# A five-branch decoder trunk on one core: differential attention ahead of sparse attention, selection rounds spread over both, a signed softmax bias, and paired scores chained in issue

## Chip, core and metric

The kernel runs on one core of a Trainium2 chip. The metric is the device time of one execution in microseconds (us), from the first to the last instruction and what lies around them. The engines are TensorE (PE, with its weight loads as PEld), VectorE (DVE), ScalarE (ACT), GpSimd (POOL) and SyncE (SP, which only issues transfers here).

## The reference, cut to what matters

Two layers. In each, one input projection feeds five branches of 512 tokens by 512 channels; each branch is gated, projected, scaled and summed, and one output projection is added to the residual.

```python
xn = rms_norm(h, norm_g[l])
(a_q, a_k, a_v, i_q, i_k, i_w, b_cq, b_ckv, b_kr, c_q, c_k, c_v, d_u, d_v, e_q, gates, merge) = split(xn @ w_in[l])
branches = (dsa_branch(...),     # A: 8 heads, keys chosen by top-128 of an indexer's score
            mla_branch(...),     # B: 8 heads, latent attention
            diff_branch(...),    # C: 4 head pairs, softmax0 - lam * softmax1, row norm
            sgu_branch(...),     # D: gated chunk mixing
            memory_branch(...))  # E: 4 heads on 256 memory tokens
mixed = sum(sigmoid(merge[:, :, n]) * ((o * silu(gates[:, :, n])) @ w_branch[l, n]) for n, o in enumerate(branches))
h = h + mixed @ w_out[l]
```

Branch A scores all keys with the indexer, keeps the 128 largest per query, and attends with the others masked. Its mask is used as an added tile: 0 where kept, -1e30 elsewhere.

## The kernel before, in words

**Units.** Every float32 product is made of three matmuls on a high and a low part (`three`, L453 to L455; ACT makes the high part of a weight tile at L368, DVE the low one at L371). Projections are "units" which PE works through in the order of the tokens of `ORDER`. After each `three` the unit calls `tick` with 3 x 0.43 ns a column, so a 512-column `three` advances the pacing clock by 0.66 us. By the code a unit lasts, on that clock: a gate `gX#` 10.6 us, a merge `mX#` 15.9 us, each of `a`, `f0`, `f1`, `fv`, `dv`, `du` 21.1 us, `qr`, `q0`, `q1` 4.0 us each, `k0`, `k1`, `v0`, `v1` 2.6 us each, `z` 1.3 us.

**Attention between the units.** `+x` puts a generator (an attention or the indexer) into a queue; it is resumed whenever the pacing clock has advanced by what it last yielded. `-x` runs the rest of it at once, `!x` forces deferred rows. The attentions share the queue `att`; the indexer has the queue `top`. `attend` makes, for each step (head, query block i = 3, 2, 1, 0 with 512, 384, 256, 256 score columns): scores, normalising of the step before, softmax, a pause `PACE[branch]`, transposes of the step before that, a pause, and P times V at the end of a head.

**Selection.** After its scores the indexer does, for query blocks 1, 2, 3, sixteen rounds of `max` (L1007) and `match_replace` (L1008) on 256, 384 and 512 columns, with a pause after each round. `dsa_attention` begins with `pace.finish(S["gidx"])`, which issues whatever rounds are left in one go.

**Banks and buffers.** `psm`: 4 PSUM banks for the units; `psa`: 3 banks for scores (`pS`, `pI`), transposes (`pT`, `pa`) and flips; `pso`: 1 bank for P times V. `pp`: 4 buffers for probabilities. The order on each engine is fixed when the program is built: among the instructions whose inputs and buffers it takes to be ready, the one that comes first in the program is issued, so a later unit's matmuls can go ahead of an attention step which lacks a bank.

**Paired scores.** Branch C computes two heads at once, one on partitions 0 to 63, one on 64 to 127: three matmuls for each, written alternately, into two banks (L1117). **Softmax.** `softmax_head` adds the mask and takes the row maximum in one DVE instruction (L543), turns it into the bias with a second one (L546), and ACT takes the exponential (L548).

Of the kernel before, what the change touches and what calls it, by code (L numbers as in the profile page):

```python
# [11 lines left out]
AF = mybir.ActivationFunctionType  # L12
ALU = mybir.AluOpType
# [10 lines left out]
GONE = -3e38  # L24
# [3 lines left out]
C_DU, C_DV, C_EQ, C_GATE, C_MERGE = 3172, 3684, 4196, 4708, 7268  # L28


ORDER = ("-mem gE0 !ckvt !lat +idx qr q0 !qr0 gE1 k0 v0 +mla0 mE0 q1 k1 mE1 mE2 -mla0 !qr1 v1 +mla1 mE3 a gB0 -mla1 gB1 "
         "!aq +dsa mB0 mB1 mB2 mB3 ws dv f0 z du fv -dsa !df0 +df0 f1 !oD gD0 gD1 mD0 mD1 -df0 !df1 "
         "+df1 mD2 mD3 gA0 gA1 mA0 mA1 -df1 mA3 mA2 gC0 gC1 mem mC0 mC1 mC3 mC2")
NW = 5
NB = 41
NC4 = 6
NTR = 8
NP = 4
NRAW = 4
PACE = {"E": 900.0, "B": 1200.0, "A": 1900.0, "C": 1600.0}  # L40
LAG_ROPE = 5000.0
LAG_QROPE = 10125.0
LAG_RSTD = 4000.0
# [89 lines left out]
def trunk(tc, d, out, taps=None):  # L133
    nc = tc.nc
    V, A, G, T = nc.vector, nc.scalar, nc.gpsimd, nc.tensor
# [29 lines left out]
    def small(n=1, name="sm"):  # L165
        return smp.tile([128, 8], F32, tag="sm", name=name)[:, :n]
# [9 lines left out]

    def f32(ap):
        return ap.bitcast(F32)

    def tap(name, ap):  # L180
        if taps is not None and name in taps:
            nc.sync.dma_start(taps[name], ap)
# [26 lines left out]
    for name in ("mem_norm_g", "norm_g", "sgu_b", "diff_norm_g", "mla_q_norm_g", "mla_kv_norm_g"):  # L209
        src = d[name]  # L210
        n = int(np.prod(src.shape)) // 128
# [328 lines left out]
    def softmax_head(ps, L, mask, scale):  # L540
        p = pp.tile([128, 512], F32, tag="p", name="p")
        m = small(1, "m")
        V.tensor_tensor_reduce(out=p[:, :L], in0=ps[:, :L], in1=mask, op0=ALU.add, op1=ALU.max,  # L543
                               scale=1.0, scalar=GONE, accum_out=m)
        nm = small(1, "nm")
        V.tensor_scalar(nm, m, -scale, None, op0=ALU.mult)  # L546
        s = small(1, "s")
        A.activation(p[:, :L], p[:, :L], AF.Exp, bias=nm, scale=scale, accum_out=s)  # L548
        return p, s

    def normalise(p, s, L):
# [25 lines left out]
    def attend(branch, steps, scores, norm, trans, pv, pv_rows=None):  # L577

        gap = PACE[branch]
        hist = []  # L580
# [66 lines left out]
    def layer(l, mm):  # L647
        w = d["w_in"][l]
        S = {}
# [253 lines left out]
        def ev_k(hf):  # L903
            def ev(ps):
                for m in range(2):
                    for s in range(2):
                        h = 4 * hf + 2 * m + s
                        S["kh"][h], S["kl"][h] = blk(name="kh"), blk(name="kl")
                        rows = slice(64 * s, 64 * s + 64)
                        split(S["kh"][h][rows], S["kl"][h][rows], ps[m][rows])  # L910
                        rr = slice(64, 96) if s == 0 else slice(0, 64)
                        A.activation(S["kh"][h][rr], f32(S["krh"][rr]), AF.Copy)
                        V.tensor_copy(S["kl"][h][rr], f32(S["krl"][rr]))
            return ev

        def ev_v(hf):
# [57 lines left out]
        def indexer():  # L974
            S["iqs"] = [blk(name="iqs") for _ in range(4)]
            for e in range(2):
                to_heads(S["iqs"][2 * e:2 * e + 2], nat_t(128 * e))
                yield 800.0
            S["ki"] = [blk(name="kih"), blk(name="kil")]
            split(S["ki"][0], S["ki"][1], nat_t(256))  # L980
            S["kk"] = [blk(name="kkh"), blk(name="kkl")]
            yield 800.0
            split(S["kk"][0], S["kk"][1], nat_t(384))
            yield 800.0
            S["mb"] = [None] * 4
            for i in (1, 2, 3):
                L = 128 * (i + 1)
                sc = S["mb"][i] = blk(F32, "score")
                for hh in range(4):
                    ps = psa("pI")  # L990
                    q = S["iqs"][hh][:, i * 128:(i + 1) * 128]
                    T.matmul(ps[:, :L], q, S["ki"][0][:, :L], start=True, stop=False)
                    T.matmul(ps[:, :L], q, S["ki"][1][:, :L], start=False, stop=True)
                    rl = tr(name="relu")
                    A.activation(rl[:, :L], ps[:, :L], AF.Relu)
                    V.scalar_tensor_tensor(out=sc[:, :L], in0=rl[:, :L], scalar=S["iw"][:, i, hh:hh + 1],
                                           in1=cm[:, 512 - 128 * i:640] if hh == 0 else sc[:, :L],
                                           op0=ALU.mult, op1=ALU.add)
                    yield 900.0
                tap(f"score{l}_{i}", sc[:, :L])  # L1000
            S["iqs"] = S["ki"] = None
            for i in (1, 2, 3):
                L = 128 * (i + 1)
                sc = S["mb"][i]
                for _ in range(16):
                    m8 = small(8, "m8")
                    V.max(out=m8, in_=sc[:, :L])  # L1007
                    V.match_replace(out=sc[:, :L], in_to_replace=m8, in_values=sc[:, :L], imm_value=GONE)  # L1008
                    yield 1500.0 + 3.0 * L
                V.tensor_scalar(sc[:, :L], sc[:, :L], -2e38, NEG, op0=ALU.is_gt, op1=ALU.mult)  # L1010

        S["qs"] = [None] * 8
# [92 lines left out]
        def diff_attention(hf):  # L1105
            sc = 64 ** -0.5
            X = S[f"df{hf}"]

            def scores(e, i):
                L = 128 * (i + 1)  # L1110
                N = max(256, L)
                q = slice(i * 128, i * 128 + 128)
                pss = [psa("pS") for _ in range(2)]
                rows = [slice(64 * s, 64 * s + 64) for s in range(2)]
                for n, (a, b) in enumerate(((0, 0), (0, 1), (1, 0))):
                    for ps, r in zip(pss, rows):
                        T.matmul(ps[:, :N], X["q"][e][a][r, q], X["k"][e][b][r, :N], start=n == 0, stop=n == 2)  # L1117
                return lambda: [softmax_head(ps, L, cm[:, 512 - 128 * i:640], sc) for ps in pss]

            def norm(ps_, e, i):  # L1120
                L = 128 * (i + 1)
                (p0, s0), (p1, s1) = ps_
                r0, r1 = small(1, "r0"), small(1, "r1")
                V.reciprocal(r0, s0)
                V.reciprocal(r1, s1)
                V.tensor_tensor(out=r1, in0=r1, in1=nlam[:, l:l + 1], op=ALU.mult)
                V.tensor_scalar(p1[:, :L], p1[:, :L], r1, None, op0=ALU.mult)
                V.scalar_tensor_tensor(out=p0[:, :L], in0=p0[:, :L], scalar=r0, in1=p1[:, :L],
                                       op0=ALU.mult, op1=ALU.add)

            def pv_rows(e, i):
                o = pso()
                for kb in range(i + 1):
                    for part in range(2):
                        T.matmul(o[:, :256], pf[part][:, kb * 384 + i * 128:kb * 384 + i * 128 + 128],  # L1135
                                 X["v"][kb][:, e].rearrange("p z c -> p (z c)"),
                                 start=(kb == 0 and part == 0), stop=(kb == i and part == 1))
                on = X["o"].setdefault(e, [None] * 4)
                on[i] = rows = tr(name="don")
                A.activation(rows[:, 128:256], o[:, 128:256], AF.Copy)  # L1140
                V.tensor_tensor(out=rows[:, :128], in0=o[:, :128], in1=rows[:, 128:256], op=ALU.add)
                ss = small(1, "dss")
                A.activation(rows[:, 128:256], rows[:, :128], AF.Square, accum_out=ss)
                r = rstd_of(ss, 1, RMS_EPS, 128.0, "dr")
                V.tensor_scalar(rows[:, :128], rows[:, :128], r, None, op0=ALU.mult)

            def flip(e):
                p = psa("pN")
                for i in range(4):
                    T.transpose(p[:, i * 128:(i + 1) * 128], X["o"][e][i][:, :128], ident)  # L1150
                oT["C"][2 * hf + e] = blk(F32, "oC")
                A.activation(oT["C"][2 * hf + e], p, AF.Copy, scale=dgain[:, l:l + 1])

            X["o"] = {}
            yield 2500.0
            yield from attend("C", causal_steps(range(2)), scores, norm,
                              lambda ps_, e, i: transposes(ps_[0][0], i), flip, pv_rows)

# [172 lines left out]
        last_l = l == DEPTH - 1  # L1331
        for tok in ORDER.split():
            c, a = tok[0], tok[1:]
# [12 lines left out]
            elif c == "g":  # L1346
                gates(a[0], (int(a[1]),))
            elif c == "m":
                merges(a[0], (int(a[1]),), last=a[0] == "C")
            elif tok == "qr":  # L1350
                gen_qr()
            elif c == "q":
# [92 lines left out]
    mm = mm0 = {"rows": memt}  # L1445
    plan.append(lambda: None)
    for l in range(DEPTH):
        mm = layer(l, mm)
# [50 lines left out]
```

## Time and profile before

| what | value |
|---|---|
| median of 3 runs | 1834.18 us (1834.01 to 1834.73) |
| the profiled execution, its own time | 1825.94 us |
| its span, first to last instruction | 1823.9 us |
| PE busy | 1774.7 us, 97% of the span |
| DVE busy | 1179.6 us, 65% |
| ACT busy | 944.0 us, 52% |
| POOL busy | 67.7 us, 4% |
| mean granted clock of TensorE | 0.996 |

PE is the engine to watch: whatever does not shorten its stream of matmuls or its gaps doesn't shorten the run. Matmuls overlap, so the time that one takes out of the stream is the distance from its start to the next one's start, not its own length.

### The profile page before, as it was taken

Reading aid. Unit: us, or ns where it says so; the run is one execution under the profiler, and the core shown is the slowest. Engines: PE = TensorE matmul, PEld = TensorE weight load, DVE = VectorE, ACT = ScalarE, POOL = GpSimd, SP = SyncE. Lnnn points to the kernel's source line nnn. Section 1 sums busy time; section 2 is a strip of 40 time slices with the busy share of each in tenths; the row PEclk is TensorE's granted clock in tenths of the full one; section 3 lists DMA queues with packets and bytes.
Section 4 is the critical chain, followed back from the end, with each engine's and each line's share of the span. In section 5 each row is a group of like instructions: output and inputs, shape, how many; then the busy total and the mean of one; then the engine's idle time right before and its main releaser. Section 6 shows DMA issues by size and latency. Waiting matters only on the chain.

```text
span 1823.9 us, 24819 instructions
## 1 busy us (share of the span) xinstructions
PE 1774.7 (97%) x8793; PEld 1470.2 (81%) x8793; DVE 1179.6 (65%) x3009; ACT 944.0 (52%) x2127; POOL 67.7 (4%) x133
## 2 busy tenths in 40 slices
PE   7999999999999999999999999999999999999998
PEld 6877778788887878888887878787888878788887
DVE  7549987955747566446465599888557575654544
ACT  7447665655645444234354467556556453442333
POOL 1000000000000001000000000010000000000000
PEclk9999999999999999999999999999999999999999
DMA  7222223132222223332352322232222222223331
GB/s 237 75 72 59 70 76 93 58 93 70 70 81 70 83 78 96 103 116 93 127 174 58 76 61 76 77 97 64 76 81 70 70 81 81 70 82 105 115 127 70
DMA packets 151588, 161.02 MB, mean 88 GB/s; under 512 B 26292, under 2 KB 130792, under 8 KB 151464
## 3 DMA queue, kind: packets, MB, share of 16 engines
q1 hardware_dynamic: 148520, 149.21, 27.6%
q0 software_dynamic: 2944, 10.23, 1.7%
q8 instruction: 69, 1.13, 0.3%
q14 instruction: 55, 0.45, 0.1%
HBM read 155.22 MB, written 4.19 MB: 87 GB/s over the span
## 4 chain that ended last, share of the span: by engine, by line
PE 93%; DVE 4%; ACT 1%; issue 1%; DMA 0%; SPq 0%; POOL 0%; POOLq 0%; DVEq 0%; ACTq 0%
PE pm L453 27%; PE pm L454 26%; PE pm L455 26%; PE po L573 2%; PE pT L563 2%; PE pS L1117 2%; PE po L1135 1%; DVE wl L371 1%; PE pa L526 1%; PE pS L455 1%; PE pS L454 1%; PE pS L453 1%; DVE score L1008 1%; PE pS L1050 1%; PE pa L1022 1%
## 5 line engine op out<-in xcount | busy, mean ns | idle before, releaser
L371 DVE TENSOR_TENSOR wl<-raw,wh 128x512 fp32r<-128x512 f32 x556 | 376.1, 681 | 350.0 <-ACT wh L368 335.5
L368 ACT ACTIVATE wh<-raw 128x512 fp32r<-128x512 f32 x556 | 345.9, 625 | 438.6 <-PE pm L454 278.2
L453 PE MATMUL pm<-xh,wh 128*128 128x512 f32 x1040 | 412.6, 397 | 2.7 <-DVE sg L1278 2.5
L454 PE MATMUL pm<-xl,wh 128*128 128x512 f32 x1040 | 407.8, 392 | 0.0
L455 PE MATMUL pm<-xh,wl 128*128 128x512 f32 x1040 | 407.5, 392 | 0.0
L453 PEld LDWEIGHTS pm<-xh,wh 128*128 128x128 f32 x1040 | 195.3, 188 | 44.6 <-DVE sg L1278 3.1
L455 PEld LDWEIGHTS pm<-xh,wl 128*128 128x128 f32 x1040 | 195.2, 188 | 40.7
L454 PEld LDWEIGHTS pm<-xl,wh 128*128 128x128 f32 x1040 | 195.6, 188 | 37.4 <-issue 1.0
L453 PE MATMUL pm<-wh,xh 128*128 128x512 f32 x512 | 202.7, 401 | 0.0
L454 PE MATMUL pm<-wl,xh 128*128 128x512 f32 x512 | 202.2, 396 | 0.0
L455 PE MATMUL pm<-wh,xl 128*128 128x512 f32 x512 | 200.9, 394 | 0.0
L548 ACT ACTIVATE p<-p,nm 128x512 f32<-128x512 f32 (+1 forms) x192 | 107.2, 558 | 82.3 <-DVE nm L546 77.7
L453 PE MATMUL pm<-yh,wh 128*128 128x512 f32 x320 | 127.2, 397 | 3.9 <-DVE acc L1304 3.9
L454 PE MATMUL pm<-yl,wh 128*128 128x512 f32 x320 | 125.9, 393 | 0.0
L455 PE MATMUL pm<-yh,wl 128*128 128x512 f32 x320 | 125.8, 393 | 0.0
L453 PEld LDWEIGHTS pm<-wh,xh 128*128 128x128 f32 x512 | 96.1, 188 | 20.2 <-issue 2.2
L455 PEld LDWEIGHTS pm<-wh,xl 128*128 128x128 f32 x512 | 96.2, 188 | 19.3
L454 PEld LDWEIGHTS pm<-wl,xh 128*128 128x128 f32 x512 | 96.4, 188 | 17.9
L185 ACT ACTIVATE pth<-pT 128x512 fp32r<-128x512 f32 (+3 forms) x176 | 78.6, 448 | 60.4 <-PE pT L563 47.0
L186 DVE TENSOR_TENSOR ptl<-pT,pth 128x512 fp32r<-128x512 f32 (+3 forms) x176 | 88.3, 503 | 33.1 <-ACT pth L185 32.5
L543 DVE CUSTOM_DVE_ANT_0 p<-pS,cm 128x128 f32<-128x128 f32 (+3 forms) x144 | 66.3, 460 | 36.0 <-PE pS L455 21.7
L554 ACT ACTIVATE p<-p,r 128x512 f32<-128x512 f32 (+3 forms) x128 | 71.6, 559 | 24.7 <-DVE r L553 24.4
(343 smaller groups left out, 2913.1 us busy)
## 6 DMA issues: line engine op xcount, KB each, us to landing
raw<-w_in SPq DMA_DIRECT2D x176, 512.0 KB, 3.6
raw<-w_branch SPq DMA_DIRECT2D x40, 512.0 KB, 3.6
raw<-w_in SPq DMA_DIRECT2D x36, 256.0 KB, 3.1
raw<-mem_w_kv SPq DMA_DIRECT2D x16, 512.0 KB, 4.6
raw<-w_out SPq DMA_DIRECT2D x16, 512.0 KB, 3.8
raw<-mla_w_uq SPq DMA_DIRECT2D x18, 128.0 KB, 2.8
xrow<-x SPq DMA_DIRECT2D x4, 512.0 KB, 6.8
raw<-mla_w_ukv SPq DMA_DIRECT2D x16, 128.0 KB, 2.5
```

What stands on the lines that cost most here:

```text
L185: A.activation(hi, src, AF.Copy)
L186: V.tensor_tensor(out=lo, in0=src, in1=f32(hi), op=ALU.subtract)
L368: A.activation(hv, raw, AF.Copy)
L371: V.tensor_tensor(out=lv, in0=raw, in1=f32(hv), op=ALU.subtract)
L453: T.matmul(o, ah, bh, start=st, stop=False)
L454: T.matmul(o, ah, bl, start=False, stop=False)
L455: T.matmul(o, al, bh, start=False, stop=sp)
L543: V.tensor_tensor_reduce(out=p[:, :L], in0=ps[:, :L], in1=mask, op0=ALU.add, op1=ALU.max, scale=1.0, scalar=GONE, accum_out=m)
L548: A.activation(p[:, :L], p[:, :L], AF.Exp, bias=nm, scale=scale, accum_out=s)
L554: A.activation(p[:, :L], p[:, :L], AF.Copy, scale=r)
L563: T.transpose(ps[:, kb * 128:(kb + 1) * 128], p[:, kb * 128:(kb + 1) * 128], ident)
L573: T.matmul(o[:, q0:], v, pf[part][:, kb * 384 + q0:kb * 384 + 512], start=(kb == 0 and n == 0), stop=(kb == 3 and n == len(ts) - 1))
```

## The change

Six things, and nothing else:

- `ORDER`: differential attention (`+df0`, `+df1`) now follows latent attention, with units gB1, fv, mB0 to mB3, f1, ws, dv, a, z, du under it; sparse attention (`+dsa`) comes after it, under gD, mD, gC and mC; branch A's gate and merges are the last of the layer instead of branch C's.
- `PACE["A"]`: 1500 ns instead of 1900 ns.
- Each selection round pauses 3000 + 8 L ns instead of 1500 + 3 L ns.
- `softmax_head`: L543 yields the negated, scaled scores and their minimum, which is the bias; L546 is gone; the exponential has scale -1.
- `ev_k`: the copy of the low rotary rows goes from DVE to ACT.
- `diff_attention.scores`: each of the six matmuls of a pair must be issued behind the one before it (no semaphore, only the order on PE).

```diff
-ORDER = ("-mem gE0 !ckvt !lat +idx qr q0 !qr0 gE1 k0 v0 +mla0 mE0 q1 k1 mE1 mE2 -mla0 !qr1 v1 +mla1 mE3 a gB0 -mla1 gB1 "
-         "!aq +dsa mB0 mB1 mB2 mB3 ws dv f0 z du fv -dsa !df0 +df0 f1 !oD gD0 gD1 mD0 mD1 -df0 !df1 "
-         "+df1 mD2 mD3 gA0 gA1 mA0 mA1 -df1 mA3 mA2 gC0 gC1 mem mC0 mC1 mC3 mC2")
+ORDER = ("-mem gE0 !ckvt !lat +idx qr q0 !qr0 gE1 k0 v0 +mla0 mE0 q1 k1 mE1 mE2 -mla0 !qr1 v1 +mla1 mE3 gB0 f0 -mla1 gB1 "
+         "fv !df0 +df0 mB0 mB1 f1 mB2 -df0 !df1 +df1 mB3 ws dv a z du -df1 "
+         "!oD !aq +dsa gD0 gD1 mD0 mD1 mD2 mD3 gC0 gC1 mC0 mC1 mC2 -dsa mC3 gA0 gA1 mem mA0 mA1 mA3 mA2")
-PACE = {"E": 900.0, "B": 1200.0, "A": 1900.0, "C": 1600.0}
+PACE = {"E": 900.0, "B": 1200.0, "A": 1500.0, "C": 1600.0}
+    def behind(ins, prev):
+        if prev is not None:
+            tc.add_manual_dep(ins.ins, prev.ins.name, mybir.DependencyInfo(
+                mybir.DependencyClass.NoSync, mybir.DependencyReason.DATA), reason="behind")
 # softmax_head
-        V.tensor_tensor_reduce(out=p[:, :L], in0=ps[:, :L], in1=mask, op0=ALU.add, op1=ALU.max,
-                               scale=1.0, scalar=GONE, accum_out=m)
-        nm = small(1, "nm")
-        V.tensor_scalar(nm, m, -scale, None, op0=ALU.mult)
+        V.tensor_tensor_reduce(out=p[:, :L], in0=ps[:, :L], in1=mask, op0=ALU.add, op1=ALU.min,
+                               scale=-scale, scalar=-GONE, accum_out=m)
-        A.activation(p[:, :L], p[:, :L], AF.Exp, bias=nm, scale=scale, accum_out=s)
+        A.activation(p[:, :L], p[:, :L], AF.Exp, bias=m, scale=-1.0, accum_out=s)
 # ev_k
-                        V.tensor_copy(S["kl"][h][rr], f32(S["krl"][rr]))
+                        A.activation(S["kl"][h][rr], f32(S["krl"][rr]), AF.Copy)
 # indexer
-                    yield 1500.0 + 3.0 * L
+                    yield 3000.0 + 8.0 * L
 # diff_attention.scores
+                prev = None
-                        T.matmul(ps[:, :N], X["q"][e][a][r, q], X["k"][e][b][r, :N], start=n == 0, stop=n == 2)
+                        mm = T.matmul(ps[:, :N], X["q"][e][a][r, q], X["k"][e][b][r, :N], start=n == 0, stop=n == 2)
+                        behind(mm, prev)
+                        prev = mm
 # the order of tokens
-                merges(a[0], (int(a[1]),), last=a[0] == "C")
+                merges(a[0], (int(a[1]),), last=a[0] == "A")
```

## Rows read from the trace of the kernel before

**Rows 1.** The page: busy time by engine, and the chain's shares.
```profile
PE 1774.7 (97%) x8793; PEld 1470.2 (81%) x8793; DVE 1179.6 (65%) x3009; ACT 944.0 (52%) x2127; POOL 67.7 (4%) x133
...
PE 93%; DVE 4%; ACT 1%; issue 1%; DMA 0%; SPq 0%; POOL 0%; POOLq 0%; DVEq 0%; ACTq 0%
```

**Rows 2.** Busy time by stretch; columns PE, PEld, DVE, ACT, POOL, clock, DMA.
```profile
150.00:353.00 203.00, 189.83 (x946) 156.33 (x945) 176.79 (x478) 127.16 (x272) 5.20 (x6) 1.00 0.27 78
353.00:545.00 192.00, 190.85 (x942) 159.49 (x941) 118.63 (x314) 111.52 (x253) 2.96 (x4) 1.00 0.26 75
545.00:700.00 155.00, 155.00 (x743) 121.08 (x742) 101.93 (x325) 73.54 (x193) 8.03 (x13) 1.00 0.25 75
```

**Rows 3.** Waits of PE, 200 to 360 us: total, times, longest.
```profile
PE pm L453 <- DVE acc L1304: 2.5, 2, 1.9
PE po L573 <- DVE ptl L186: 1.6, 2, 1.4
PE po L573 <- ACT pth L185: 1.6, 1, 1.6
PE pm L453 <- DVE sg L1278: 1.1, 1, 1.1
PE pm L453 <- ACT mth L1293: 1.0, 1, 1.0
PE pS L1050 <- DVE qs L965: 0.8, 1, 0.8
```

**Rows 4.** The chain in order of time, 340 to 360 us: start, length, what.
```profile
348.19 0.69 DVE score L1008
...
349.48 0.60 DVE m L1007
350.11 0.69 DVE qs L965
```

**Rows 5.** Two short stretches at the lower clock, columns as in rows 2.
```profile
351.50:355.00 3.50, 3.28 (x12) 2.96 (x11) 3.10 (x10) 1.35 (x3) 0.00 (x0) 0.51 0.00 0
...
1252.60:1256.00 3.40, 3.40 (x11) 2.71 (x12) 3.16 (x8) 0.84 (x2) 0.00 (x0) 0.50 0.00 0
```

**Rows 6.** DVE time of L1007 and of L1008 in the first stretch.
```profile
150.00:353.00 203.00, 26.39 (x48) 1.00 0.27 78
...
150.00:353.00 203.00, 29.31 (x96) 1.00 0.27 78
```

**Rows 7.** Timeline of PE, 552 to 692 us: score runs that go alone.
```profile
553.03 0.44 PE L1117 MATMUL pS<-kh,qh 64*128 64x384 f32 x1
...
555.02 0.40 PE L454 MATMUL pm<-wl,xh 128*128 128x512 f32 x1
555.25 0.40 PE L455 MATMUL pm<-wh,xl 128*128 128x512 f32 x1
555.58 0.38 PE L1117 MATMUL pS<-kh,qh 64*128 64x256 f32 x1
...
556.46 0.40 PE L455 MATMUL pm<-wh,xl 128*128 128x512 f32 x1
...
691.55 0.39 PE L1117 MATMUL pS<-kh,qh 64*128 64x256 f32 x1
```

**Rows 8.** Timeline of PE, 575.5 to 577.4 us: a pair of 384 issued together.
```profile
575.63 0.39 PE L455 MATMUL pm<-wh,xl 128*128 128x512 f32 x1
575.95 0.44 PE L1117 MATMUL pS<-kh,qh 64*128 64x384 f32 x2
...
577.00 0.39 PE L454 MATMUL pm<-wl,xh 128*128 128x512 f32 x1
```

**Rows 9.** Three lines by their instructions: count, ns min/median/max, first and last start.
```profile
L546 DVE TENSOR_SCALAR nm<-m x192: 133/147/157, 187.5 to 1599.2; 128x1 f32<-128x1 f32 x192
...
L913 DVE CAST kl<-krl x16: 407/410/420, 179.3 to 1139.5; 32x512 fp32r<-32x512 f32 x8, 64x512 fp32r<-64x512 f32 x8
...
L912 ACT ACTIVATE kh<-krh x16: 626/630/635, 177.3 to 1141.3; 32x512 fp32r<-32x512 f32 x8, 64x512 fp32r<-64x512 f32 x8
```

**Rows 10.** Line L1117 from 540 to 700 us, the first layer's scores.
```profile
L1117 PE MATMUL pS<-kh,qh x32: 337/386/501, 546.6 to 691.5; 64*128 64x256 f32 x16, 64*128 64x512 f32 x8, 64*128 64x384 f32 x8
```

## Prediction

> **What bounds the kernel now.** I read the page first. PE is busy for 97% of the span and holds 93% of the chain that ended last; DVE and ACT have room on average [rows 1]. So a part of this change is worth what it takes out of PE's stream of matmuls or out of PE's gaps, and nothing else. Next I cut the span by stage [rows 2]. The first layer's stretch from 150 to 353 us (latent attention, indexer and selection) is the poor one: PE stands for 203 - 189.8 = 13.2 us of it, and DVE is busy for 176.8 of 203 us, 87%. From 353 to 545 us (sparse attention) DVE is at 62%, from 545 to 700 us (differential attention) at 66%, and PE stands for 1.1 us and for nothing. The second layer repeats the pattern 901 us later (1252.6 against 351.5 us [rows 5]). PE's waits between 200 and 360 us then name who is late [rows 3]: DVE or ACT results each time, 8.6 us in all. I leave the waits between 150 and 200 us alone, since hardly a selection round has run by then. The chain in order of time shows the worst place, just where sparse attention starts [rows 4]: between the DVE instructions that PE waits for (L965, the query parts) lie L1008 and L1007, a selection round that had not been finished. Around it stand the wait for `pth` (1.6), for `qs` (0.8), for `sg` (1.1) and 0.2 of `ptl`, 3.7 us together [rows 3], and right behind it PE runs at half clock (1.2 instead of 2.4 GHz) for 3.4 us, in both layers [rows 5], which costs another 1.7 us. I call these 5.4 us a layer the cluster. The rest of rows 3 is 4.9 us (`acc`, `ptl`, `mth`).
>
> **The selection rounds, and the order.** A layer's rounds take 26.4 + 29.3 = 55.7 us of DVE, all inside the first stretch, 27 of its 87 points [rows 2, 6]. By the code they are paced over 16 x (2268 + 2652 + 3036) ns = 127 us of the pacing clock, behind 13 us of indexer scores: 140.5. The units from `+idx` to `+dsa` give 138.7 (96.4 up to mE3, a 21.1, gB0 and gB1 10.6 each). So the last round is left over and is issued in one go, as the chain shows [rows 4]. After the change the rounds ask for 16 x (5048 + 6072 + 7096) ns = 291.5, with the scores 304.7; the units up to `+dsa` give 309: 96.4, two gates, f0, fv, f1, dv, a, du at 21.1 each, four merges at 15.9 and z at 1.3. They fit with 4 us over, so nothing is left to finish there. One us of the pacing clock was 1.29 us of the trace in the second stretch (192 us for 149) and 1.46 us in the first (203 for 139); at 1.37, the rounds spread over about 400 us, 14 points of DVE instead of 27. That gives 74% in the stretch of latent attention and 66 + 14 = 80% in that of differential attention, which now carries the rounds: less than the 87% at which PE stands, more than the 62 to 66% at which it does not.
>
> What this is worth can't be read off exactly. Bounds from rows: all of the 8.6 us and the half-clock stretch, 10.3 us a layer, on one side; on the other side the waits move along with the rounds (a rival below). I take the cluster as gone, because its place goes: behind latent attention now come gB1 and 42 us of units before any scores need fresh queries, and at the new `+dsa` the projection du lies between `a` and its use. Of the other 4.9 us I take half, since DVE keeps half of the rounds there. That is 5.4 + 2.4 = 7.8 us. Against it I set 3 us a layer of new waits at 80%, nearer to the rows without waits than to the row with them. Net 4.8 us a layer, 9.6 us in all.
>
> **The chained scores.** The 256-column scores of one head go alone [rows 7]: from the matmul ahead (555.25) to the second behind (556.46) are 1.21 us, less two places of 0.23 us (555.02 to 555.25): a lone run takes 0.75 us of PE. Three places of 256 columns are 3 x 0.12 (half of 0.23), so 0.39 us is lost on going in and out. A pair issued together (`x2`) takes for 384 columns 577.00 - 575.63 - 0.46 = 0.91 us [rows 8]: three places of 0.17 and again 0.39, for both heads. By the timeline all sixteen runs of 256 columns of a layer go alone (the first and the last are shown, with the count [rows 7, 10]), three of the four pairs of 384 columns are apart too, and the four of 512 together. If each of these eleven pairs went together, a layer would gain 8 x 0.75 + 3 x 0.91 = 8.7 us, both 17.5 us. But the pairs are written alternately already; when the second head comes late, it has no bank or buffer yet, and a chain makes neither. Then the first matmul goes out alone, and the other five follow when the bank is there, two heads at a time: 0.12 + 0.39, and 0.75 for the five in three places, 1.26 us instead of 1.50; for 384 columns 0.17 + 0.39 + 0.91 = 1.47 instead of 1.82. That saves 8 x 0.24 + 3 x 0.35 = 3.0 us a layer, 6 us in all. The lower bound is nothing: the four pairs of 512 and the whole one of 384, if they came apart in the new company, would give back 4 x 0.62 + 0.56 = 3.0 us. I take 6.
>
> The row shows the 0.39 us; the Trainium skill (TensorEngine Tiling (Array Packing), Key Properties) says that changing the tiling mode drains TensorE, which is a rule against cutting a pair once more. By it, as by the row, a pair cut in two drains twice before and after, and only places are saved.
>
> **The small parts.** L546 is 192 x 147 ns = 28 us of DVE [rows 9]; L543 stays one instruction over the same elements. I cost it at nothing directly: PE's other work covers softmax. Without this cover it would be 0.15 us a head on the way to the exponential. The copy in `ev_k` leaves DVE (0.41 us, 16 times) for ACT, where its twin L912 takes 0.63 us [rows 9]. Queued behind it on ACT are the next heads' high parts, which the score matmuls wait for: between nothing and 8 x 0.63 = 5 us a layer; I take nothing, because units run under it. `PACE["A"]` makes 76 pauses of 1.5 us, 114 us, under units of 153 us; before 144 under 149. Differential attention asks for about 54 us a half under 69 and 80 us. So no attention has a rest to be run at once, and branch A's gate, now last, finds its input made one merge earlier; without that margin a head's P times V would stand before gA0. On SP the weight loads come in the new order of the units, with the same four loads ahead; no wait of PE in rows 3 is for a transfer. On POOL the loads of the mixing weights and the row norms of `lr` now lie among the reciprocal roots of differential attention; one that lacks a block holds those up, and the flip of that head after them. The spare 15 and 26 us of the two halves cover it.
>
> **The sum.** -9.6 (waits) - 6 (scores) = -15.6 us against the profiled 1825.94 us (1823.9 of span and 2 around it): 1810.3. The median of the runs is 1834.18, 8.2 above the profiled execution; I carry the difference over: 1818.6, so 1818.
>
> **Rivals.**
> - All pairs go together, because the chain holds a bank until both have one: 17.5 instead of 6 gives 1834.2 - 27.1 = 1807. For it: 512 columns pair always. Against: in rows 7 unit matmuls lie between the lone runs, so the second head was late.
> - The waits move with the rounds. If what PE loses grows evenly from 66% (none) to 87% (13.2 us in 203), then 80% over some 220 us costs 9.5 us and 74% in the first stretch 5.0: 14.5, as much as the 13.2 + 1.7 of before. Only the scores remain: 1828.
> - Slower: DVE in the stretch of differential attention comes out as full as the first one was, 87%. Then 13.2 x 220 / 203 = 14.3 us stand there, 5.0 in the first, and the cluster's 5.4 come back at `+dsa`: 24.7 against 14.9, +9.8 a layer, with the scores' -6 the time is 1848. It decides from about 18 us of waits a layer on. For it: norms, row norms and rounds meet in one queue; against: 62 to 66% without them.
> - Slower, another way: the chain lets unit matmuls in between, so that each of the six goes alone at 0.51 to 0.62 us instead of a third of a run: 8 x 1.56 + 3 x 1.54 + 2.45 + 4 x 2.64 = 30 us a layer, 1885. Against: the three matmuls of one head also depend on each other in order, and in rows 7 they are issued back to back.
>
> **How the numbers follow.** Forecast 0.5 (its own range 1809 to 1828), all pairs together 0.15, waits move 0.2, full DVE 0.1, opened chain 0.05. From the top, 1848 and 1885 are left out, and a little of the best case, 0.18 together: 1802 to 1836. Below 0.2% (3.7 us) a measurement of this kernel hardly tells a difference. Faster by more: nearly all of the forecast, the paired case and 0.12 of the moved waits, 0.76; within it 0.11; slower 0.13.
>
> **What would show it.** Selection rounds ending some 20 us at most before the first sparse scores, at about 560 us; DVE near 74% and 80% in the two stretches; PE idle from 200 to 360 us down to some 3 us, without half clock around 350 us; score runs of one and of five (or six) instead of three; no L546. The prediction is wrong if PE waits for `ptl`, `don` or a `pm` bank in the stretch of differential attention by more than about 8 us a layer, if another half-clock stretch shows up, or if L1117 is still issued in threes.

## The result, and the profile after

The median went from 1834.1 us (four executions, 1832.26 to 1834.73) to 1821.07 us (four, 1820.71 to 1821.17): the ratio is 0.993, with an interval of 0.9913 to 0.9947. The forecast was 1818. The profiled executions say something else: 1825.94 before, 1820.71 after, spans 1823.9 and 1818.8, only 5.1 us apart. The total came out near the forecast, its terms did not. In what follows PE "stands" when none of its matmuls is running, and "half clock" is 1.2 instead of 2.4 GHz.

The page after the change, busy time by engine and the chain's shares:

```profile
PE 1769.3 (97%) x8793; PEld 1467.0 (81%) x8793; DVE 1158.0 (64%) x2801; ACT 953.0 (52%) x2143; POOL 65.7 (4%) x133
...
PE 94%; DVE 4%; ACT 1%; issue 1%; DMA 0%; SPq 0%; POOL 0%; POOLq 0%; DVEq 0%; ACTq 0%
```

Against [rows 1], PE is busy for 5.4 us less, and span less busy time is 49.5 us instead of 49.2: PE stands as long as before, only elsewhere. Busy time by stretch shows where; the columns are those of [rows 2], and the last two lines are short windows inside the second stretch:

```profile
150.00:353.00 203.00, 196.38 (x984) 162.61 (x983) 152.34 (x386) 133.43 (x285) 0.00 (x0) 1.00 0.26 73
353.00:560.00 207.00, 200.13 (x980) 158.74 (x979) 152.69 (x429) 99.19 (x256) 19.16 (x29) 0.98 0.28 81
520.00:545.00 25.00, 19.27 (x90) 15.95 (x89) 22.89 (x66) 10.37 (x29) 4.62 (x7) 0.89 0.30 84
539.40:546.10 6.70, 3.16 (x13) 2.86 (x14) 6.70 (x26) 3.25 (x10) 0.55 (x1) 0.50 0.28 78
```

In the first stretch PE stands for 6.6 us where it stood for 13.2 [rows 2], and DVE is at 75%. In the stretch of differential attention, which had 1.1 us of standing when sparse attention was there, PE now stands for 6.9 us, and for 6.7 us it gets half the clock. The second layer does the same: 11.5 to 6.7 us, and 1.3 to 6.9.

PE's waits from 200 to 360 us, and then from 360 to 600 us; total, times, longest, as in [rows 3]:

```profile
PE pm L459 <- ACT mth L1300: 1.0, 1, 1.0
PE pm L459 <- DVE acc L1311: 0.6, 1, 0.6
PE pm L459 <- DVE ql L192: 0.2, 1, 0.2
...
PE pz L459 <- ACT vnh L191: 5.6, 1, 5.6
PE pm L459 <- ACT nat L1019: 1.1, 1, 1.1
PE pz L460 <- DVE vnl L192: 0.2, 1, 0.2
```

The 8.6 us of [rows 3] are 1.8 (in the second layer 8.5 became 2.8), and the whole cluster is gone: no `pth`, `qs`, `sg` or `ptl`. In its place stands one wait of 5.6 us, at `z`, the mixing product of branch D. PE's timeline there (start, length, what; in brackets the wait):

```profile
536.93 0.28 PE L1142 MATMUL po<-dv,ptl 128*128 128x256 f32 x1
542.79 0.79 PE L459 MATMUL pz<-vnh,wsh 128*128 128x256 f32 x2 [5.58 <-ACT vnh L191]
543.74 0.58 PE L460 MATMUL pz<-vnl,wsh 128*128 128x256 f32 x1 [0.15 <-DVE vnl L192]
```

And DVE's timeline of the same time:

```profile
536.67 0.54 DVE L1215 TENSOR_SCALAR sguv<-sguv,mv,lr 128x512 f32<-128x512 f32 x1
...
537.20 0.67 DVE L1012 MATCH_REPLACE8 score<-m,score 128x512 f32<-128x512 f32 x1
537.80 0.68 DVE L377 TENSOR_TENSOR wl<-raw,wh 128x512 fp32r<-128x512 f32 x1
538.39 0.28 DVE L1152 TENSOR_SCALAR don<-don,dr 128x128 f32<-128x128 f32 x1
538.59 0.68 DVE L377 TENSOR_TENSOR wl<-raw,wh 128x512 fp32r<-128x512 f32 x1
539.19 0.68 DVE L1216 TENSOR_TENSOR sguv<-sguv,lng 128x512 f32<-128x512 f32 x1
539.79 0.28 DVE L1148 TENSOR_TENSOR don<-po,don 128x128 f32<-128x128 f32 x1
540.00 0.28 DVE L314 TENSOR_TENSOR rope<-nat,cP 128x128 f32<-128x128 f32 x1
...
541.61 0.68 DVE L1217 TENSOR_TENSOR sguv<-sguv,lnb 128x512 f32<-128x512 f32 x1
```

L1215, L1216 and L1217 are the last three steps of one block of the row norm that `z` reads. From the start of the first to the start of the last are 4.94 us, of which the two in front take 1.06 (0.46 and 0.60, from start to next start) and other work 3.88: half a selection round 0.67, two weight splits 1.19, differential rows 0.41, rope rows 0.94, another block's low part 0.67. The timeline shows no rest of DVE in between. PE's order is fixed, and `z` comes right behind the projections, so it stands. The whole row norm can be measured from the last copy of dv's product out of PSUM (L1199) to the start of the last step (L1217): the last times of these lines, first in the changed kernel, then in e4, a run below with fast rounds:

```profile
L1199 ACT ACTIVATE sguv<-pm x4: 587/598/599, 505.1 to 510.6; 128x512 f32<-128x512 f32 x4
...
L1217 DVE TENSOR_TENSOR sguv<-sguv,lnb x4: 676/681/691, 522.9 to 541.6; 128x512 f32<-128x512 f32 x4
...
L1199 ACT ACTIVATE sguv<-pm x4: 588/598/600, 508.2 to 513.3; 128x512 f32<-128x512 f32 x4
...
L1217 DVE TENSOR_TENSOR sguv<-sguv,lnb x4: 674/682/685, 523.0 to 538.0; 128x512 f32<-128x512 f32 x4
```

That is 31.0 us, and 24.7 with fast rounds; in the kernel before it was 20.6. In the 31.0 us DVE spends 2.5 on selection and 6.0 on weight splits (from start to next start), in the 24.7 nothing and 4.3. So the rounds themselves are the smaller part of the 6.3 us between the two; the rest is other work that is queued there along with them, and DVE's idle time.

The scores, in PE's timeline of one pair of 256 columns, against the lone runs of three in [rows 7]:

```profile
405.59 0.39 PE L459 MATMUL pm<-yh,wh 128*128 128x512 f32 x1
405.91 0.38 PE L1122 MATMUL pS<-kh,qh 64*128 64x256 f32 x1
406.22 0.50 PE L460 MATMUL pm<-yl,wh 128*128 128x512 f32 x1
406.56 0.40 PE L461 MATMUL pm<-yh,wl 128*128 128x512 f32 x1
406.88 0.38 PE L1122 MATMUL pS<-kh,qh 64*128 64x256 f32 x1
406.88 0.50 PE L1122 MATMUL pS<-kl,qh 64*128 64x256 f32 x2
407.11 0.39 PE L1122 MATMUL pS<-kh,ql 64*128 64x256 f32 x2
407.43 0.39 PE L1142 MATMUL po<-dv,pth 128*128 128x256 f32 x1
```

One matmul goes alone, five follow together. The lone one costs 406.56 - 405.59 - 0.46 = 0.51 us, as forecast; runs of five cost 0.75 to 0.76. Of the 16 pairs of 256 columns in both layers, 14 are issued so. Worked out in this way run by run, the differential scores took 45.8 us of PE before and 38.6 after, in both layers: 7.2 us less.

### The profile page after: what moved, and what is told of

It reads as the page before. It is cut to its first block, busy times and chain, and to the rows that moved or that the text cites. A ratio compares the mean times of both kernels' runs of the same rounds, so it can differ in the third digit from the quotient of the medians.

```text
span 1818.8 us, 24673 instructions
## 1 busy us (share of the span) xinstructions
PE 1769.3 (97%) x8793; PEld 1467.0 (81%) x8793; DVE 1158.0 (64%) x2801; ACT 953.0 (52%) x2143; POOL 65.7 (4%) x133
## 4 chain that ended last, share of the span: by engine, by line
PE 94%; DVE 4%; ACT 1%; issue 1%; DMA 0%; SPq 0%; POOL 0%; POOLq 0%; DVEq 0%; ACTq 0%
PE pm L459 27%; PE pm L460 27%; PE pm L461 27%; PE pT L567 2%; PE po L577 2%; PE pS L1122 2%; PE po L1142 1%; DVE wl L377 1%; PE pS L461 1%; PE pa L1026 1%; PE pS L460 1%; PE pS L459 1%; PE pa L532 1%; PE pS L1055 1%; PE pS L1054 1%
## 5 line engine op out<-in xcount | busy, mean ns | idle before, releaser
L552 ACT ACTIVATE p<-p,m 128x512 f32<-128x512 f32 (+1 forms) x192 | 107.1, 558 | 90.3 <-DVE m L549 89.9
```

The costliest lines, as they stand in the source:

```text
L552: A.activation(p[:, :L], p[:, :L], AF.Exp, bias=m, scale=-1.0, accum_out=s)
```

## The experiments

There are three theories. **Z**: what was won at the old place of sparse attention is lost again at `z`, since its row norm (on DVE, between the units dv and `z`) lies behind the selection rounds in DVE's queue on a short way. **Rounds**: the gain of the first stretch comes from the rounds being spread, so faster rounds bring those waits back. **Chain**: the chained scores bring what they save in PE's stream. Each comparison is with runs of the kernel before on the same chip, whose median was 1831.63 (e1 to e4), 1830.35 (e5 to e8) and 1832.35 us (e10 to e13).

**e1: `z` further from dv.** The last merge of branch B moves between them.

```diff
-... !df1 +df1 mB3 ws dv a z du -df1
+... !df1 +df1 ws dv a mB3 z du -df1
```

> The changed kernel with one token moved: mB3 stands between a and z instead of ahead of ws. If the 5.6 us wait of each layer's first mixing matmul (pz, for the high part of the normed rows vnh) comes from the short way between dv and z, the 16 us of units more make it vanish, with the half-clock stretch behind it (6.8 us at half clock, 3.4 us lost): 9 us a layer, 18 in all, about 1803 us. Rival: DVE is too full in this stretch and the wait only moves to another unit: 1815 to 1821 us.

Measured: 1833.78 us (1830.36 to 1835.66), ratio 1.0018 (1.0006 to 1.0031). All of the gain is gone, which neither the expectation nor its rival had. The timelines of ACT and PE:

```profile
544.75 1.32 ACT L191 ACTIVATE vnh<-sguv 128x256 fp32r<-128x256 f32 x4
...
546.05 0.39 PE L461 MATMUL pm<-yh,wl 128*128 128x512 f32 x1
...
549.63 0.39 PE L459 MATMUL pz<-vnh,wsh 128*128 128x256 f32 x1 [2.32 <-ACT mth L1300]
```

The first four of the eight high parts of the row norm's result are made at once at 544.75, as the last merge's matmuls on `yh` come to their end (546.05), though the row norm's last step began on DVE at 523.9 us. They and the merge's `yh`, `yl` live in one pool of six buffers (`NC4`). So e1 changed more than the distance, and does not test theory Z. Two more runs go after that: **e10** is e1 with eight such buffers (`NC4` 6 to 8; to make room the block pool `NB` goes from 41 to 38), **e13** is the changed kernel with the same two sizes.

> The run with mB3 between a and z, with eight c4 buffers instead of six and 38 blocks instead of 41 (the room for it). In that run the first normed row (vnh) was made at 544.7 us, 26 us after the last row norm, while mB3's last matmul ran at 546. If the c4 buffers held it up, it is now made soon after its row norm, near 520 us, PE no longer waits around z, and the time falls by 10 us or more against that run's 1833.8: 1815 to 1823 us. Rival: DVE's full queue holds it up; nothing moves, 1830 to 1835 us.

> The control for it: the changed kernel with eight c4 buffers and 38 blocks. Here branch B's gated rows are used up at 479 us, before the row norms start, so the buffers hold nothing up, and the 5.6 us wait at z stays: 1821 us. Rival: three blocks fewer delay the latent heads, 1824 us or more; or the buffers were the cause of the wait here too, and the time falls to 1805 us.

e13 came out as the changed kernel did: 1820.62 us, ratio 0.9942 (0.9923 to 0.9962), with the same 5.6 us wait; the sizes alone do nothing. e10 stays where e1 was: 1834.44 us (1826.67 to 1839.51), ratio 1.0011 (0.9996 to 1.0027). ACT's timeline in e10:

```profile
510.52 0.42 ACT L191 ACTIVATE vnh<-sguv 128x256 fp32r<-128x256 f32 x1 [0.54 <-DVE sguv L1217]
...
526.44 0.42 ACT L191 ACTIVATE vnh<-sguv 128x256 fp32r<-128x256 f32 x1 [0.42 <-DVE sguv L1217]
...
542.52 1.34 ACT L191 ACTIVATE vnh<-sguv 128x256 fp32r<-128x256 f32 x4
```

With two buffers more, four of the eight pieces are made 16 to 32 us ahead of the other four (the first and the last of them are shown), which are still late: the buffers did hold them. But the time did not follow, though PE has no wait at `z` any more; it waits 3.2 us for `qs` and 2.3 for the parts of P instead, in a profiled execution of 1826.67 us that lies below the median. So taking the wait away at `z` is not enough in every order, and why this one is slow is left open.

**e5: row norm early.** f1 is moved behind dv, the merges of branch B ahead of it, and sparse attention starts after gD0 and gD1.

```diff
-"fv !df0 +df0 mB0 mB1 f1 mB2 -df0 !df1 +df1 mB3 ws dv a z du -df1 "
-"!oD !aq +dsa gD0 gD1 mD0 mD1 ...
+"fv !df0 +df0 mB0 mB1 mB2 mB3 ws dv f1 -df0 !df1 +df1 a z du !oD gD0 gD1 -df1 "
+"!aq +dsa mD0 mD1 ...
```

> The changed kernel, rounds as slow as in it, with another order: mB0 to mB3 stand together ahead of ws and dv, then f1 and a lie between dv and z (42 us of units instead of 21), and gD0, gD1 are under the second half of differential attention. Theory: mB3 behind a (the run before) could not help, since branch B's gated rows hold four of the six c4 buffers until mB3 is done and the normed rows (vnh, vnl) need four; here they are free early, so the 5.6 us wait of pz and the half-clock stretch behind it vanish: 9 us a layer, about 1803 us. Rival: DVE's row in this stretch (differential rows, row norms and rounds in one queue) is what makes PE wait, whatever the token order; the waits move and the time stays at 1815 to 1825 us.

Measured: 1811.08 us (1807.11 to 1811.73), ratio 0.9891 (0.9874 to 0.9909). Busy time by stretch:

```profile
353.00:560.00 207.00, 205.35 (x988) 162.59 (x986) 148.90 (x409) 96.39 (x240) 15.16 (x22) 1.00 0.29 83
520.00:545.00 25.00, 24.20 (x136) 18.30 (x135) 22.53 (x91) 17.59 (x59) 1.65 (x3) 1.00 0.15 43
```

And a line each of ACT's and PE's timeline:

```profile
492.66 0.73 ACT L191 ACTIVATE vnh<-sguv 128x256 fp32r<-128x256 f32 x2 [2.87 <-DVE sguv L1217]
...
533.71 0.39 PE L459 MATMUL pz<-vnh,wsh 128*128 128x256 f32 x1
```

The last high parts are there at 493 us, 40 us ahead of their use; the wait and the half clock are gone in this layer, and PE stands for 1.7 us instead of 6.9. In the second layer it stands for 1.6 us, but a half-clock stretch of 3.4 us is left among the matmuls of `z` (at 1428 us). DVE is still at 90% from 520 to 545 us (22.5 of 25): not the share made PE stand, but what was queued late. The 18 us expected were not reached. In the traces PE stands for 10.8 us less than in the changed kernel and is busy for 1.2 more: the score runs take 43.1 us of PE instead of 38.6. One more pair a layer, of 512 columns, comes apart, for some 0.65 us each; the rest are runs that begin behind a short wait (up to 0.4 us) or stand next to transposes and P times V. The edit moves several units at once, so this is not the distance alone.

**e4: fast rounds.** The changed kernel with the old pauses, `yield 1500.0 + 3.0 * L`.

> The changed kernel with the pauses of before (1500 + 3 L) behind each selection round; the rounds end about 140 us of the pacing clock behind their start and no longer run under differential attention. If the spread rounds are what took PE's waits away between 200 and 360 us, some 5 us a layer come back there; if they are also what makes the normed rows late for z, the 9 us a layer there go: 1821 + 10 - 18 = 1813 us. Rival, the wait at z is a matter of the order alone: 1831 us.

Measured: 1812.93 us (1809.37 to 1816.06), ratio 0.9901 (0.9882 to 0.992). The time is as expected, its parts are not. Busy time in the first stretch and around `z`:

```profile
150.00:353.00 203.00, 193.86 (x963) 160.29 (x962) 172.89 (x444) 131.84 (x282) 0.00 (x0) 0.99 0.25 73
520.00:545.00 25.00, 23.85 (x127) 20.06 (x126) 21.88 (x64) 14.22 (x40) 5.35 (x8) 1.00 0.29 85
```

PE's waits from 200 to 360 us (0.2 for `ql` is left out):

```profile
PE pm L459 <- ACT mth L1300: 0.9, 1, 0.9
PE pm L459 <- DVE acc L1311: 0.9, 1, 0.9
PE pT L567 <- ACT p L558: 0.9, 1, 0.9
PE pm L459 <- DVE sg L1285: 0.9, 1, 0.9
```

From 360 to 600 us PE now waits 1.1 us in all, at `z` (0.8 and 0.3), and the half clock is gone there, so theory Z stands by a second, different edit as to the place and the short way; of the rounds it is true only in part, since they fill 2.5 us of that way. The row norm's result is there 3.0 us sooner than in the changed kernel, and PE comes to `z` 2.2 us later. But DVE is at 85% in the first stretch, nearly the 87% of before, and PE waits 3.8 us there, not 8.6: more than half of the relief came without spreading (no round is left over ahead of sparse attention in the new order), and spreading adds 2.0 us in the first layer. Theory Rounds is right in sign, and the smaller share.

**e8, e11: the same question in e5's order.** e8 has the old pauses, e11 has `2000.0 + 5.0 * L`.

> The order of the run with f1 between dv and z, and the fast rounds of before, which then run under latent attention alone. If both the rounds in the queue and the short way to z were needed for the wait, this is no better than either alone, 1803 us; if fast rounds alone leave 4 to 5 us a layer around z (as they did in the changed order), this one takes these away too: 1803 to 1806 us. Rival: fast rounds bring back waits under latent attention now that they are done early: 1812 us.

> The order with f1 between dv and z, with pauses between those of before and after: 2000 + 5 L. With slow rounds it took 1811.1 us, with fast ones 1816.1 us (waits and half-clock stretches between 150 and 200 us). If the queue of DVE sets both ends, the middle lies at 1808 to 1813 us. Rival: only the planner's order matters, and it may come out anywhere from 1805 to 1820 us.

e8: 1816.05 us, ratio 0.9922 (0.9903 to 0.994), slower than expected and than its rival. e11: 1811.75 us, ratio 0.9894 (0.9874 to 0.9914), as e5. With nothing late at `z`, fast rounds cost: in e8 PE waits 3.2 us for `sg` between 150 and 360 us, and half clock appears at 187 us for 6.8 us, in a profiled execution of 1819.85 us that lies above the median; e4 has the same waits there without that stretch. By the medians, spreading the rounds is worth some 5 us where the row norm is early and costs some 8 where it is late.

**e2, e3, e12: the chain.** e2 is the kernel before plus the chain alone; e3 is the changed kernel without it; e12 is e5 without it (the edit of e3 and e12; e2 has it the other way round).

```diff
-                        mm = T.matmul(ps[:, :N], ...)
-                        behind(mm, prev)
-                        prev = mm
+                        T.matmul(ps[:, :N], ...)
```

> The kernel before with nothing but the issue chain on the six matmuls of a pair. By the prediction's working the lone runs of three become runs of one and five, and 3.0 to 3.7 us a layer leave PE's stream, 6 to 7.5 us in all: about 1827 us. Rival: the chain counts only in the new order, and here it gives nothing (1834 us), or all pairs go together (1817 us).

> The changed kernel without the issue chain. If the chain is worth what its score runs took less in the trace (7.3 us), this one takes 1828 us, and L1117 is issued in threes again. Rival: the new order alone brings the pairs together, and without the chain the time stays at 1821 us.

> The order with f1 between dv and z, slow rounds, without the issue chain. In this order the chained runs took 43.1 us of PE's stream in both layers, hardly less than the 45.8 of the kernel before. If the chain's worth is only what it saves in runs of scores, this one is 0 to 3 us slower than 1811.1 us. Rival, by the run without the chain in the changed order (4 us faster than with it): the chain costs more in waits than it saves, 1805 to 1808 us.

e2: 1825.45 us, ratio 0.9975 (0.9963 to 0.9987); its scores take 42.1 us instead of 45.8. In the old order the chain saves 3.7 us in PE's stream, and by the ratio it is worth 4.6 us. e3: 1816.73 us (1811.47 to 1821.52), ratio 0.9922 (0.9898 to 0.9947): expected slower, it came out not slower than the changed kernel, and perhaps faster, though its scores take 41.4 us. PE's timeline shows that the stop has moved:

```profile
536.80 0.39 PE L461 MATMUL pm<-wh,xl 128*128 128x512 f32 x1
540.79 1.12 PE L1154 MATMUL pN<-ident,don 128*128 128x128 f32 x4 [3.60 <-DVE don L1149]
...
542.41 0.56 PE L459 MATMUL pz<-vnh,wsh 128*128 128x256 f32 x1
```

PE comes free at the same time as in the changed kernel, waits 3.6 us for the differential rows, and by then the row norm is ready. The chain changes PE's issue order everywhere, and here the stop is shorter without it. e12: 1811.96 us (1806.0 to 1813.13), ratio 0.9882 (0.9854 to 0.991), the same as e5, although its scores take 45.6 us instead of 43.1. So theory Chain holds for the stream and in the old order; in the new orders its net is not told apart from the reordering.

**e6, e7: the small parts.** e6 is the changed kernel with the maximum and L546 back; e7 has the copy in `ev_k` back on DVE.

> The changed kernel with the two-step softmax bias of before (row maximum, then L546's 0.15 us on one column). Costed at nothing: 1821 us, DVE 28 us more busy. Rival: in the full DVE queue of 520 to 545 us the added instructions make the normed rows for z later still, some 1 us a layer: 1823 us or more; or the planner's new order moves waits by a few us either way.

> The changed kernel with the copy of the low rotary rows back on DVE. Costed at nothing: 1821 us. Rival: 8 copies of 0.63 us a layer less in front of the first latent scores on ACT give up to 5 us a layer (1811 us), or DVE's 8 x 0.41 us more cost up to 3 us a layer (1827 us).

e6: 1820.51 us (1819.08 to 1822.99), ratio 0.995 (0.9932 to 0.9968): no worth of the new bias shows. e7: 1823.46 us (1822.84 to 1825.43), ratio 0.9966 (0.9954 to 0.9978): by the medians the copy on ACT is worth about 2 us. In e7 PE waits 3.7 us in all for gates (`sg`, made by DVE) instead of 1.5. It also has a half-clock stretch at 184 us, but so has e13, where the copy is on ACT. `PACE["A"]` was not undone by itself; what it is worth is not shown.

## Why the forecast came out right in the total and wrong in its terms

**The relief of the first stretch: right.** 7.8 us a layer were forecast. PE's standing there fell by 6.6 and 4.8 us, and the two half-clock stretches of [rows 5], 1.7 us each by the prediction's count, are gone: 8.3 and 6.5. The cluster went for the reason given, its place is gone; e4, without the spreading, has no wait for `pth`, `qs` or `ptl` there either. The last selection instruction starts at 549.6 us, 32 us ahead of the first sparse scores at 581.6: nothing was left to finish, though both numbers are off from the 20 and 560 us of the forecast.

**The new waits: the step that failed.** "3 us a layer of new waits, spread, at 80%". DVE was at 74% in that stretch, lower than forecast, and yet 6.9 us of waits stood there, nearly all at one place, and 6.7 us at half clock, in which PE was busy for 3.2 us, so some 1.6 more: 8.5 us a layer. So the term of the waits, -9.6 us by the forecast, came to about nothing: 14.8 us won in the first stretches, and 17.0 us in the second ones, where 2.4 had stood before. A stretch's mean share of DVE was taken as the measure of its waits. e4 (85% and 3.8 us in the first stretch) and e5 (90% around `z` and no wait there) show that it isn't one. What decided here is the way from a result to the unit that must have it, dv to `z` with only a between them, and what DVE had queued in it, weight splits more than rounds. The prediction named the place, "norms, row norms and rounds meet in one queue", but in the rival for a full DVE, which did not come. Of what it said would prove it wrong, one sign came (another half-clock stretch) and one stayed just below its bound (6.9 of 8 us, and at `vnh`, which it had not listed).

**The chained scores: the form right, the size only with help from the order.** 6 us were forecast and 7.2 measured in the stream, in the form given: runs of one and five, and 512 columns stayed together. (That the second head lacks a bank is the reason given; no run tests it.) But the chain alone does not bring this: it saves 3.7 us in the old order (e2), and in the new one the scores take 41.4 us without it (e3) and 38.6 with it, so 2.8 of the 7.2 are the chain's and 4.4 came with the rest of the change. That the term came near its size is luck. The all-together rival was nearest in e3, where six pairs of 256 columns go as one run of six without any chain. The fixed 0.39 us on entering and leaving came out at much the same for the other lengths: 0.76 us for five of 256 columns, less three places of 0.12, leaves 0.40; 1.12 us for six of 512, less three places of 0.23, leaves 0.43. The rule quoted from the Trainium skill (TensorEngine Tiling (Array Packing), Key Properties), that a change of tiling mode drains TensorE, fits: a run of five costs no more than one of three, and what is saved is places.

**The small parts: the copy was mis-sized.** Nothing was taken for it; e7 shows about 2 us of gain. The likely reason, argued from the waits for `sg` and not tested, is that DVE, 16 times 0.41 us shorter, has the gates sooner. On ACT the copy takes 0.61 us, about as its twin in [rows 9], and PE's waits show no head's high part that came late for it. The bias at nothing was right (e6), L543's successor taking as long as before.

**The sum, and the carried difference: two errors that cancel.** Against the profiled 1825.94 the terms gave -15.6; measured are -5.2. In the page's numbers: standing unchanged (+0.3), stream -5.4, of which -7.2 are the scores, and the half clock around `z` gives 2 x 1.6 back; these make -3.7 with the standing, and 1.4 us stay unassigned. Apart from the end and from `z`, both profiled executions have three half-clock stretches of 3.4 us, after the change at 1000, 1058 and 1082 us: those of [rows 5] went, others came. Then 8.2 us were carried over, the distance of before's median from its profiled execution. After the change that distance is 0.4. The kernel before runs between 1825.92 and 1835.04 us from execution to execution. In the 23 executions beside e1 to e4, those at a mean granted clock of 0.996 took 1826.05 to 1826.7 us, those at 0.989 to 0.990 took 1831.7 to 1834.3. The profiled one is of the first kind, so its profile shows the least half clock seen in this kernel. All four executions of the changed kernel stand at 0.993. So of the -13.0 between the medians the traces explain 5.2. The other 7.8 goes, by the pattern of the later executions, with a lower granted clock in executions of before that left no trace, and which places of it the change took away can't be shown. The -13.0 is also at the upper end: the median of the 52 later executions of before is 1831.72, 10.7 us above the changed kernel's, and e13 lies 11.7 below its own comparison. Two errors that cancel, the waits' -9.6 that did not come and a distance of 8.2 that vanished, brought the total near 1818 (the sum gives 1818.6): that is luck.

**The rivals.** The full DVE did not come (75 and 74%), nor did the opened chain. "Waits move with the rounds" is the nearest in substance: standing of the same length in another place, though by one late result and not by a share of DVE. It gave 1828 with the carried difference and 1820 without it, and the profiled execution took 1820.71, where the forecast's terms give 1810.3.

**Best version.** e5, e11 and e12 lie at 1811 to 1812 us, below both kernels; none of their executions took longer than 1814.12 us, and none of the changed kernel's less than 1820.71. e4, at 1812.93, is not told apart from them.

## What to carry to other kernels

Where work is moved on a shared engine, look up for each result that the bound engine must have in order how far its producer lies ahead and what is queued in between; here a mean busy share of a stretch said neither that PE would wait nor that it wouldn't. A saving in PE's stream and a wait elsewhere are one sum, so undo each part alone: a gain in the stream (the chain) can be lost to the reordering that it brings. And before a difference between median and profile is carried over, see whether it belongs to the kernel: it went from 8.2 to 0.4 us here.

## What had not been expected of the hardware

Executions of the kernel before differ by 0.5% (1825.92 to 1835.04 us), the slower ones at a lower mean granted clock (0.996 down to 0.989), while the changed kernel, with its longer single waits (5.6 us), repeated to within 0.5 us in four executions and to 2.5 us in e13's four. PE went to half clock at 539.3 us, 2.1 us into that wait, and stayed there for 6.8 us; in e3 a wait of 3.6 us at the same place went with 6.8 us as well (539.2 to 546.0), and in e6, waits of 3.3 and 1.4 us there with 3.4 us. So the wait's price is not its length alone.
